# Splitting one output store into 112 + 4 + 4 + 4 + 4 rows in a linear-attention kernel on one core

## The chip, the core and the metric

The kernel runs on one core of a Trainium2 chip. Five engines work side by side: PE (TensorE, matrix multiplies; PEld is its weight load), DVE (VectorE), ACT (ScalarE), POOL (GpSimd) and SP (SyncE). SP, ACT and POOL also issue DMA transfers, and all transfers of the core run on the same 16 DMA engines. The metric is the time of one execution on the device, in microseconds (us).

## The reference

For 8 x 12 = 96 heads of 512 positions and 64 features, all float32, it computes linear attention with a ReLU feature map:

```python
Q_feat = np.maximum(0, Q)
K_feat = np.maximum(0, K)
KV = np.einsum('bhkd,bhkv->bhdv', K_feat, V)
K_sum = np.sum(K_feat, axis=2)
numerator = np.einsum('bhqd,bhdv->bhqv', Q_feat, KV)
denominator = np.einsum('bhqd,bhd->bhq', Q_feat, K_sum)
return (numerator / (denominator[:, :, :, None] + 1e-10)).astype(np.float32)
```

Q, K and V are 12.58 MB each, 37.75 MB read in all, and the output is 12.58 MB.

## The kernel before

**Tiling.** Heads are taken eight at a time: an "octet", and there are NO = 12 of them, numbered by `o`. A quantity of one octet is 1 MB in float32. K and V of an octet come as two groups of four heads, each a tile of 128 partitions x 16 rows x 64 features; Q of an octet is one tile of 128 partitions x 32 rows x 64. The output tile `o_sb` of an octet is 128 partitions x 32 rows x 64 in float32, so one partition ("row" of the transfer) holds 2048 numbers, 8 KB, which are contiguous in DRAM.

**Loads.** K and V of octet 0 are loaded as float32, by SP (`k_first`) and ACT (`v_first`), into two buffers of the pool of output tiles. All other loads are issued by POOL in the order Q0, K1, V1, Q1, K2, V2, Q2 ... and turn float32 into bf16 on the way (lines 94 and 106). They have their own buffers, and each POOL load waits until an earlier one has landed, so that some eight are under way at a time.

**Compute.** Per group DVE makes the ReLU of K (`kf`, line 138) and copies of V (`vo`, lines 140, 147; ACT does some, line 145). PE multiplies them into `ps_kv` (line 152), ACT moves the result to `kvd` (line 162). Q is transposed on PE (line 173), ACT applies the ReLU (line 181). PE makes the denominators (line 212) and the transposed numerators (line 203), ACT copies these (line 205), PE transposes them back (line 230), and DVE multiplies by the reciprocals and writes `o_sb` (line 236). `backs(o)` is that last part for octet `o`, and it ends in `store(o, o_sb)`.

**Stores.** All stores are issued by SP (line 249, and line 247 for the last octet, whose store is cut in two halves along the free axis). SP works its instructions off in order. With `DELAY = 6`, store `o` of the first six octets also waits for the landing of K load `o + 6` (line 251): it is kept back so that the loads come first. The pool `outp` has DELAY + 2 = 8 buffers, so the tile of octet 8 takes the buffer of octet 0 (two of the eight were used first by `k_first` and `v_first`), and its writer has to see that octet 0's store has landed. The order of all instructions is the order in which the program text issues them (`manual_schedule`); a framework adds the semaphores.

Of the kernel before, what the change touches and what calls it, by code (L numbers as in the profile page):

```python
# [10 lines left out]
def kernel(  # L11
# [7 lines left out]
    nc = tc.nc  # L19
    B, H, S, D = Q.shape  # L20
    assert D == 64
    P = 128
# [9 lines left out]
    NO = NG // 2  # L32
    assert NO * 8 == NH and R == 16 and RQ == 32
    DELAY = 6
# [54 lines left out]
    k_load = {}  # L89
    after_load = mybir.DependencyInfo(mybir.DependencyClass.Sync, mybir.DependencyReason.DATA)  # L90
# [151 lines left out]
    def store(o, o_sb):  # L242
        Ov = Or[o].rearrange("p (r d) -> p r d", d=D)
        if o == NO - 1:
            for j in range(2):
                rs = slice(RQ // 2 * j, RQ // 2 * (j + 1))
                nc.sync.dma_start(out=Ov[:, rs], in_=o_sb[:, rs])
            return
        st = nc.sync.dma_start(out=Ov, in_=o_sb)
        if o + DELAY < NO:  # L250
            tc.add_manual_dep(st.ins, k_load[o + DELAY].ins.name, after_load, reason="store after load")

    def out_tile():
        return outp.tile([P, RQ, D], fp32, name="o_sb", tag="o_sb")
# [19 lines left out]
    def backs(o):  # L274
        o_sb = out_tile()
        for j in range(2):
            norm(o, j, back(o, j), o_sb)
        store(o, o_sb)
# [26 lines left out]
    o = NO - 2  # L305
# [10 lines left out]
    o_sb = out_tile()  # L316
# [4 lines left out]
    for i in range(2):  # L321
        relu_q(o + 1, i, transp(o + 1, i), nc.vector if i == 1 else None)
    norm(o, 1, ps, o_sb)
    store(o, o_sb)
    idle(5, o + 1)
    out_t(o + 1, (0,))
# [32 lines left out]
```

## Time and profile before

| What | Value |
|---|---|
| Median of 3 runs | 127.03 us (126.72 to 127.13) |
| The profiled execution | 127.0 us, of which the span of the instructions is 125.2 |
| Busy: PE, PEld, DVE, ACT, POOL | 85.0, 76.9, 81.0, 79.0, 23.7 us |
| DMA | 10139 packets, 32.66 MB on the core's side |
| Queue q0 (POOL's loads) | 74.1% of 16 engines' span |
| Queue q1 (SP: first K load and all stores) | 27.1% |
| Queue q8 (instruction fetches) | 8 packets |
| One 1024 KB store, issue to landing | 8.9 us in the median |

The page divides the span into 40 slices; a digit is the busy share in tenths. "DMA" is the mean share over the 16 DMA engines. [...] A DMA transfer raises a semaphore 16 times, once for each DMA engine, and "landed" means that all 16 have come.

### The profile page before, as it was taken

The page shows a single profiled execution, that of the slowest core. Times are in us where ns is not written, and L with a number is a line of the kernel's source. Part 1 is how long each engine was busy: PE and PEld are TensorE (multiplying, and loading weights), DVE is VectorE, ACT ScalarE, POOL GpSimd, SP SyncE. Part 2 cuts the span into 40 slices and gives each one's busy share as a digit, 9 for nine tenths or more (in the row PEclk, how much of TensorE's full clock was granted, in tenths as well). Part 3 has the DMA queues.
Part 4 walks back from the last instruction along what each step waited for, and adds up shares of the span by engine and source line. Part 5 has one row for each costly group of instructions (what it writes and reads, how often), then busy time and mean ns, then how long its engine had stood idle before and what let it go on. Part 6 is the DMA issues. An engine that isn't in the chain of part 4 may idle for free.

```text
span 125.2 us, 2614 instructions
## 1 busy us (share of the span) xinstructions
PE 85.0 (68%) x1067; PEld 76.9 (61%) x1067; DVE 81.0 (65%) x176; ACT 79.0 (63%) x114; POOL 23.7 (19%) x40
## 2 busy tenths in 40 slices
PE   0000547898989979898966985955997597797600
PEld 0000547796878879787855983943975595775500
DVE  2006963679889797979859349449549409978610
ACT  0003737999899898989877576845499095547000
POOL 6922124221242213322121130210000000000000
PEclk9999999999999999999999599996899869999996
DMA  3999999999999999999999999999999999999991
GB/s 92 365 306 229 215 209 211 213 211 217 207 217 208 211 213 211 214 273 311 214 247 341 210 222 342 234 217 325 258 215 305 279 215 307 425 419 419 432 403 73
DMA packets 10139, 32.66 MB, mean 261 GB/s; under 512 B 784, under 2 KB 784, under 8 KB 8720
## 3 DMA queue, kind: packets, MB, share of 16 engines
q0 software_dynamic: 7712, 17.83, 74.1%
q1 hardware_dynamic: 2144, 13.63, 27.1%
q10 hardware_dynamic: 272, 1.05, 2.2%
q8 instruction: 8, 0.13, 0.4%
q14 instruction: 3, 0.02, 0.0%
HBM read 37.75 MB, written 12.58 MB: 402 GB/s over the span
## 4 chain that ended last, share of the span: by engine, by line
DVE 37%; DMA 28%; PE 19%; ACT 7%; issue 3%; DVEq 1%; ACTq 0%
DMA v_sb<-in_V_dram 20%; DVE o_sb L236 15%; PE ps_kv L152 10%; DMA k_first<-in_K_dram 7%; DVE kf L138 7%; PE ps_bk L230 7%; DVE vo L140 4%; ACT kvd L162 3%; DVE vo L147 3%; DVE den L220 2%; PE ps_qt L173 2%; DVE rec L224 2%; DVE own L215 2%; ACT qt L181 2%; ACT vo L145 1%
## 5 line engine op out<-in xcount | busy, mean ns | idle before, releaser
L152 PE MATMUL ps_kv<-vo,kf 128*128 128x132 bf16 x384 | 30.2, 240 | 19.9 <-ACT vo L145 13.8
L152 PEld LDWEIGHTS <-kf 128*128 128x128 bf16 x384 | 27.4, 107 | 21.6 <-DVE vo L140 12.9
L236 DVE TENSOR_TENSOR o_sb<-ps_bk,rec 128x1024 f32<-128x1024 f32 x24 | 28.3, 1219 | 13.6 <-PE ps_bk L230 13.6
L162 ACT CAST kvd<-ps_kv 64x260 bf16<-64x260 f32 (+1 forms) x54 | 18.6, 345 | 16.6 <-PE ps_kv L152 13.9
L205 ACT COPY ot_sb<-ps_ot 128x1024 f32<-128x1024 f32 x24 | 24.1, 1013 | 6.8 <-PE ps_ot L203 5.9
L230 PE MATMUL ps_bk<-ident,ot_sb 128*128 128x128 f32 x192 | 23.4, 276 | 0.4 <-ACT ot_sb L205 0.4
L181 ACT ACTIVATE qt<-ps_qt 128x1024 bf16<-128x1024 bf16 x23 | 22.4, 1028 | 0.2
L230 PEld LDWEIGHTS ps_bk<-ident,ot_sb 128*128 128x128 f32 x192 | 21.2, 143 | 0.7 <-ACT ot_sb L205 0.7
L203 PE MATMUL ps_ot<-qt,kvd 128*128 128x256 bf16 x96 | 14.9, 283 | 9.9 <-DVE o_sb L236 9.0
L138 DVE TENSOR_SCALAR kf<-k_sb,mask 128x1024 bf16<-128x1024 bf16 x44 | 18.4, 459 | 4.5 <-DMA k_sb<-in_K_dram 4.5
L203 PEld LDWEIGHTS <-kvd 128*128 128x128 bf16 x96 | 9.2, 100 | 13.2 <-issue 11.0
L173 PE MATMUL ps_qt<-ident,q_sb 128*128 128x128 bf16 x192 | 14.7, 237 | 0.7 <-DMA q_sb<-in_Q_dram 0.7
L173 PEld LDWEIGHTS <-q_sb 128*128 128x128 bf16 x192 | 13.3, 108 | 1.4 <-DMA q_sb<-in_Q_dram 1.3
L140 DVE TENSOR_SCALAR vo<-v_sb,mask 128x1024 bf16<-128x1024 bf16 x22 | 11.0, 501 | 4.7 <-DMA v_sb<-in_V_dram 4.7
L145 ACT ACTIVATE vo<-v_sb,mask 128x1024 bf16<-128x1024 bf16 x10 | 11.5, 1154 | 2.0 <-DMA v_sb<-in_V_dram 1.8
L94 POOL DMA_DIRECT2D v_sb<-in_V_dram x11 | 8.2, 750 | 22.2 <-DMA q_sb<-in_Q_dram 9.4
L106 POOL DMA_DIRECT2D q_sb<-in_Q_dram x12 | 7.1, 588 | 20.9 <-DMA k_sb<-in_K_dram 15.3
L94 POOL DMA_DIRECT2D k_sb<-in_K_dram x11 | 7.9, 717 | 15.4 <-DMA v_sb<-in_V_dram 9.8
L212 PEld LDWEIGHTS <-qt 128*128 128x128 bf16 x192 | 6.8, 96 | 3.6 <-ACT qt L181 2.5
L212 PE MATMUL ps_den<-kvd,qt 128*128 128x16 bf16 x192 | 7.3, 180 | 1.9 <-ACT qt L181 1.7
L145 ACT ACT_TABLE_LOAD x1 | 1.3, 1283 | 11.3 <-DMA v_first<-in_V_dram 11.3
L138 DVE TENSOR_SCALAR kf<-k_first,mask 128x1024 bf16<-128x1024 f32 x4 | 2.8, 750 | 7.7 <-DMA k_first<-in_K_dram 7.7
(24 smaller groups left out, 31.8 us busy)
## 6 DMA issues: line engine op xcount, KB each, us to landing
out_dram<-o_sb SPq DMA_DIRECT2D x11, 1024.0 KB, 8.9
q_sb<-in_Q_dram POOLq DMA_DIRECT2D x12, 512.0 KB, 20.7
k_sb<-in_K_dram POOLq DMA_DIRECT2D x11, 512.0 KB, 21.8
v_sb<-in_V_dram POOLq DMA_DIRECT2D x11, 512.0 KB, 20.5
k_first<-in_K_dram SPq DMA_DIRECT2D x1, 1024.0 KB, 9.3
v_first<-in_V_dram ACTq DMA_DIRECT2D x1, 1024.0 KB, 10.5
out_dram<-o_sb SPq DMA_DIRECT2D x2, 512.0 KB, 4.5
```

The lines of the kernel that those rows point to most:

```text
L94: ld = eng.dma_start(out=t.rearrange("p g r d -> p g (r d)"), in_=X[2 * o:2 * o + 2].rearrange("g p f -> p g f"))
L138: nc.vector.tensor_scalar(kf[g][:, :, s, :], k_sb[g], scalar1=0.0, scalar2=mask[:, 0, s:s + 1], op0=Alu.max, op1=Alu.mult)
L140: nc.vector.tensor_scalar(vo[g % NB][:, :, 0, 2:D + 2], v_sb[g], scalar1=mask[:, 1, 0:1], scalar2=None, op0=Alu.mult)
L152: nc.tensor.matmul(ps_kv[:, g % 2, 0:2 * (D + 2)].rearrange("p (t d) -> p t d", t=2), kf[g][:, r, :, :].rearrange("p s d -> p (s d)"), vo[ ...
L162: copy(kvd[o % NK][64 * c:64 * c + 64, 4 * gs.start + s:4 * gs.stop:2, c * D1:c * D1 + D1].rearrange("p (g t) d -> p g t d", t=2), ps_kv[6 ...
L173: nc.tensor.transpose(ps[:, u, :], q_sb[o][:, i * (U // 2) + u, :], ident)
L181: nc.scalar.activation(to, ps, Act.Relu)
L203: nc.tensor.matmul(ps[:, i], kvd[o % NK][:, h, 1:2 * D + 1], q[:, :, h, :], start=True, stop=True, skip_group_check=True)
L205: nc.scalar.copy(ot[o][:, :, 4 * j:4 * j + 4], ps.rearrange("p h u c -> p u h c"))
L212: nc.tensor.matmul(ps[:, u], qt_sb[o % NZ][:, u, :], kvd[o % NK][:, :, 0:2 * D1:2 * D1 - 1], start=True, stop=True, skip_group_check=True)
L230: nc.tensor.transpose(ps[:, 2 * v:2 * v + 2].rearrange("p c d -> p (c d)"), ot[o][:, 8 * j + v].rearrange("p h c -> p (h c)"), ident32)
L236: nc.vector.tensor_tensor(o_sb[:, rs], ps, rec[o][:, rs].unsqueeze(2).to_broadcast([P, 16, D]), op=Alu.mult)
```

## The change

The store of octet 0 is issued as five transfers, along the partitions: rows 0 to 111, 112 to 115, 116 to 119, 120 to 123 and 124 to 127. All five carry the same wait for K load 6. The other stores are as before. A transfer's rows are divided among DMA engines: 128 rows are 8 for each of the 16, 112 rows are 7 for each of the 16, and 4 rows are 1 for each of 4 engines. By the change's description these four are engines 0 to 3, which then carry 11 rows of octet 0's store while the others carry 7. Bytes and results are the same.

```diff
@@ store()
                 rs = slice(RQ // 2 * j, RQ // 2 * (j + 1))
                 nc.sync.dma_start(out=Ov[:, rs], in_=o_sb[:, rs])
             return
-        st = nc.sync.dma_start(out=Ov, in_=o_sb)
-        if o + DELAY < NO:
-            tc.add_manual_dep(st.ins, k_load[o + DELAY].ins.name, after_load, reason="store after load")
+        cuts = [0, 112, 116, 120, 124, P] if o == 0 else [0, P]
+        for lo, hi in zip(cuts, cuts[1:]):
+            st = nc.sync.dma_start(out=Ov[lo:hi], in_=o_sb[lo:hi])
+            if o + DELAY < NO:
+                tc.add_manual_dep(st.ins, k_load[o + DELAY].ins.name, after_load, reason="store after load")
```

## The prediction

> **What bounds the kernel now.** First the page: its slices, DMA queues and chain.
>
> ```profile
> span 125.2 us, 2614 instructions
> ...
> DMA  3999999999999999999999999999999999999991
> GB/s 92 365 306 229 215 209 211 213 211 217 207 217 208 211 213 211 214 273 311 214 247 341 210 222 342 234 217 325 258 215 305 279 215 307 425 419 419 432 403 73
> ...
> q0 software_dynamic: 7712, 17.83, 74.1%
> q1 hardware_dynamic: 2144, 13.63, 27.1%
> q10 hardware_dynamic: 272, 1.05, 2.2%
> q8 instruction: 8, 0.13, 0.4%
> ```
>
> The 16 DMA engines are full from the second slice to the last but one. PE, DVE and ACT are at 63 to 68% of the span. The chain of work names DVE, DMA and PE in turn, but it ends on the last compute instruction, and the stores land after that. So I cut the end into windows:
>
> ```profile
> core 0: us, PE busy (x) PEld busy (x) DVE busy (x) ACT busy (x) POOL busy (x), PEclk, DMA share, GB/s
> ...
> 104.00:122.00 18.00, 11.13 (x140) 9.51 (x136) 12.80 (x23) 6.66 (x11) 0.00 (x0) 1.00 1.01 408
> 122.00:123.00 1.00, 0.00 (x0) 0.00 (x0) 0.00 (x0) 0.00 (x0) 0.00 (x0) 1.00 0.55 221
> 123.00:124.00 1.00, 0.00 (x0) 0.00 (x0) 0.00 (x0) 0.00 (x0) 0.00 (x0) 0.50 0.07 29
> ```
>
> From 104 to 122 us there are only stores, back to back; then the engines stop one after another. In the trace's DMA records a transfer's landing is 16 increments, one per engine: those of the last store come at 122.14, 122.20, 122.21 and 122.27 us, and so on to 123.89. The slowest DMA engine sets the end, and the first four finish 1.6 to 1.75 us before it.
>
> The records also show where that spread is from. The landing increments of a load at 25.98 us spread over 0.7 us. Then the q8 row's eight instruction fetches follow, 16 KB each, one packet of 879 to 974 ns on one engine (starts 26.95, 36.74, 47.78, 57.91, 70.58, 83.24, 98.31, 111.56). After each, one more engine lands about 0.9 to 1.1 us late and stays so: one at 29.29, two at 39.2, three at 51.66, some eight at the end.
>
> Now the store that changes, in SP's waits and then its timeline:
>
> ```profile
> SPq L249 <- DMA k_sb<-in_K_dram: 98.5, 6, 50.5
> ```
>
> ```profile
> 51.74 0.35 SPq L249 DMA_DIRECT2D out_dram<-o_sb  x1
> 61.67 0.33 SPq L249 DMA_DIRECT2D out_dram<-o_sb  x1
> ```
>
> Store 0 leaves at 51.74, as soon as K load 6 has landed (51.66), store 1 at 61.67. By the records, store 0's rows start at 55.16, 8 KB per packet, 8 per engine, alternating with load packets (309 to 322 ns a row, 154 a load packet), and it lands at 60.68.
>
> **The change part by part.** *Issues.* One DMA instruction becomes five. SP takes four more at 0.33 to 0.35 us, so 1.4 us: the fifth leaves near 53.2, before the first row moves (55.16) and 8.4 us before store 1 is due. Cost nothing; the cover is SP's wait for K load 7. POOL's queue is not touched. *Waits.* All five wait for the same K load, so the last four find it done: an event wait of 17 ns each. *Semaphores.* Landings rotate over eight in the records. Four more transfers shift the rotation, and the tightest reuse becomes the last store's (at 119.4), which needs the semaphore of store 4, landed at 100.64. Nothing waits. *Buffer.* Octet 8's multiply on DVE (92.39) reuses octet 0's tile and must see five landings, not one; they are there by about 63. At 21 ns an event wait that is 0.08 us of DVE, covered by the DMA backlog.
>
> *Rows.* This is the whole price. An engine that serves rows one after another needs 0.306 us for each (8 rows of a 1 MB store, 2.45 us between landings in the tail). Twelve engines get 7 rows for 8: -0.31 us. Engines 0 to 3 get 11: +0.92 us, if the four rows of a piece move at the speed of other rows. Four more completion packets at 22 ns add 0.09 us to each.
>
> *Do they?* Every store of before is one transfer of 128 rows, and there a row takes 309 to 322 ns. In a piece four engines at once read four neighbouring partitions, a form that the trace does not show. Lower end: fully parallel, four pieces take 4 x 0.309 = 1.24 us per engine. Upper end: neighbouring rows are served one after another, so that each piece takes 4 x 0.309 = 1.24 us and four take 4.94. The engines' extra is then between +0.92 and +4.63 us. A stretched packet does hold its engine: after the fetch at 57.91 a store row took 755 ns and the next load packet began only at its end. A reason for a gain below 0.92 I see none. I take about +2.3: four engines that collide on the first piece leave it at different times, and are then partly on different pieces, which are different partitions. It lies nearer the parallel end, where the rows I have are.
>
> [...]
>
> [...]
>
> *Sum.* Last landing of before: 123.89 in a span of 125.2, in an execution of 127.0; the median of the three runs shown is 127.03, so the sum is carried over as it is. Engines 4 to 15: 123.89 - 0.31 = 123.58. Engines 0 to 3, if they are early ones: 122.2 to 122.5 + 2.3 = 124.5 to 124.8, say 124.7. The later sets the end: +0.8 us, **127.8 us**. What is late next: the loads that land between 60 and 104 us come up to 1.4 us later, because engines 0 to 3 are now the last; compute (DVE's waits on loads of 1.6 to 2.1 us) moves with them, but it has no say in the end: the last multiply ends at 118.2 while rows are queued until 121.
>
> **The rivals.** *A. Parallel and well aimed.* Rows of a piece cost 0.31 each and all four engines are among the early ones: 122.2 to 122.6 + 1.0 = 123.2 to 123.6, the others 123.58. End -0.3: **126.7 us** (own range 126.5 to 126.9). It decides wherever engines 0 to 3 have over 1.3 us in hand and a piece takes under about 0.4 us. For it: four engines do end 1.6 us early, and 3 rows for 4 engines is just that size. Against it: it needs both conditions.
>
> *B. Parallel but badly aimed.* One of engines 0 to 3 is one of the eight late ones, which land the last store between 123.05 and 123.89. Then 123.1 to 123.9 + 0.95: **127.2 to 128.0 us**, say 127.6. The records carry no engine number. I followed each engine's packets end to start back to the first transfer, whose 16 first packets start 14 ns apart, and took that order for the numbers. Of the first four, one leads to an engine that later had a fetch (83.24 or 111.56). Through the stalls of the first microseconds that is half a coin toss.
>
> *C. Full collision.* Serial pieces: engines 0 to 3 +4.6, end 122.2 + 4.6 = 126.8, +2.9: **130 us**. Also what comes out if a piece goes to one engine, always the same. The spread-out arrival speaks against the whole of it.
>
> *D. It does not do what it says:* the rows are spread over other engines, or a third thing sets the end; 127.0, within 0.2.
>
> **How the numbers follow.** Partial collision (the forecast) 0.43, at 127.4 to 128.8; A 0.20; B 0.22; C 0.04; D 0.11. A change of 0.3% (0.38 us) is about what a measurement of this kernel can tell from none. Faster by more: 0.08 of A, whose -0.3 is at the edge, 0.04 of D: 0.12. Within: 0.12 of A, 0.05 of D, 0.05 of B, 0.04 of the forecast: 0.26. Slower: the rest, 0.62. The range leaves out C, half of A's faster half and the upper end of the forecast's: 126.6 to 129.1; the forecast's own is 127.4 to 128.8.
>
> **What would show it.** The issue list should have x10 of 1024 KB, one of 896 and four of 32. If a piece uses four engines, q1 has 2160 packets (112 + 16 completions + 4 x 8 for 128 + 16); 2208 if each uses sixteen. Collision: some 8 KB packets of q1 between 56 and 62 us that take 0.6 to 1.2 us. A well-aimed rebalance: the last store's landings within less than 1.2 us instead of 1.75. The prediction is wrong if the pieces' rows take 0.31 us, and the sign then hangs on whether engines 0 to 3 had fetches; the windows after 122 us show it as a steeper or a longer tail.

## The result, and the profile after

The changed kernel takes 127.70 us in the median of 4 runs (127.61 to 127.92), against 127.00 us for the kernel before (126.72 to 127.13, 4 runs). The ratio is 1.0061, 95% interval 1.0040 to 1.0082: slower by 0.6%, or 0.7 us. The profiled execution took 127.71 us, with a span of 125.9 us (before: 127.0 and 125.2).

The page of the changed kernel, the lines that answer to those shown of before, with two lines of its list of DMA issues (count, KB of one, median us from issue to landing):

```profile
span 125.9 us, 2620 instructions
...
DMA  3999999999999999999999999999999999999990
...
q0 software_dynamic: 7712, 17.83, 73.6%
q1 hardware_dynamic: 2160, 13.63, 26.8%
q10 hardware_dynamic: 272, 1.05, 2.2%
q8 instruction: 8, 0.13, 0.4%
q14 instruction: 3, 0.02, 0.0%
...
out_dram<-o_sb SPq DMA_DIRECT2D x2, 512.0 KB, 6.6
out_dram<-o_sb SPq DMA_DIRECT2D x1, 896.0 KB, 7.6
```

q1 has 2160 packets for 2144: each small transfer adds four completion packets, so each goes to four DMA engines. In the records a small transfer raises its semaphore not 16 times but five: once between 52.59 and 53.66 us, before any row of the store moves (55.13), and four times as its rows land (59.37 to 59.48 for the first, 61.25 to 61.41 for the last). The engines are full for as long as before. What is new lies behind the last full slice. The end of the changed kernel in windows of half a microsecond (the last two columns are the DMA share and GB/s):

```profile
122.00:122.50 0.50, 0.00 (x0) 0.00 (x0) 0.00 (x0) 0.00 (x0) 0.00 (x0) 0.50 0.78 320
122.50:123.00 0.50, 0.00 (x0) 0.00 (x0) 0.00 (x0) 0.00 (x0) 0.00 (x0) 0.50 0.45 180
123.00:123.50 0.50, 0.00 (x0) 0.00 (x0) 0.00 (x0) 0.00 (x0) 0.00 (x0) 0.50 0.12 49
123.50:124.00 0.50, 0.00 (x0) 0.00 (x0) 0.00 (x0) 0.00 (x0) 0.00 (x0) 0.50 0.04 16
```

The same two last windows of the kernel before:

```profile
123.00:123.50 0.50, 0.00 (x0) 0.00 (x0) 0.00 (x0) 0.00 (x0) 0.00 (x0) 0.51 0.14 57
123.50:124.00 0.50, 0.00 (x0) 0.00 (x0) 0.00 (x0) 0.00 (x0) 0.00 (x0) 0.50 0.00 0
```

After 123.5 us before moves nothing more. After the change something still moves at 16 GB/s and 4% of 16 engines: that is one engine, alone. In the records the last store's 16 landing increments read 122.01, 122.12, 122.44 and so on up to 123.56 and 123.57, and then one by itself at **124.35**. The other fifteen end 0.32 us before the last increment of before (123.89). So the change did most of what it says, and one of the four loaded engines spoils it.

That is +0.46 us (124.35 - 123.89), and the loss is 0.71. The rest comes after the last landing. SP ends the program by waiting for the stores' semaphores. Its waits from 118 us on, before and then after (us in total, times, longest):

```profile
SPq L354 <- DMA out_dram<-o_sb: 3.8, 3, 1.4
```

```profile
SPq L356 <- DMA out_dram<-o_sb: 6.1, 3, 3.7
```

The records give these waits an order: semaphores 108, 109, 113, 114, 115, 116, 117, 118, whatever landed last, about 0.06 us apart even where a wait finds its store done. In before the last store raises semaphore 117; SP passes it at 123.91, has one more to look at, and ends (its drain) at 124.03, 0.14 us after the landing. Four more transfers turn the rotation of eight on, and the last store raises 113. SP passes that at 124.36, must still go through 114 to 118, one by one, at 124.43, .48, .55, .61 and .67, and drains at 124.73, 0.38 us after the landing. That is +0.25 us, and 0.46 + 0.25 = 0.71.

### The profile page after: what moved, and what is told of

The parts are those of the page before. It is cut to its first block, busy times and chain, and to the rows that moved or that the text cites. A ratio compares the mean times of both kernels' runs of the same rounds, so it can differ in the third digit from the quotient of the medians.

```text
span 125.9 us, 2620 instructions
## 1 busy us (share of the span) xinstructions
PE 83.8 (67%) x1067; PEld 75.9 (60%) x1067; DVE 80.9 (64%) x176; ACT 79.1 (63%) x114; POOL 23.4 (19%) x40
## 3 DMA queue, kind: packets, MB, share of 16 engines
q1 hardware_dynamic: 2160, 13.63, 26.8%
q10 hardware_dynamic: 272, 1.05, 2.2%
## 4 chain that ended last, share of the span: by engine, by line
DVE 35%; DMA 28%; PE 22%; ACT 5%; issue 2%; DVEq 1%; ACTq 0%
DMA v_sb<-in_V_dram 21%; DVE o_sb L236 15%; PE ps_kv L152 10%; DMA k_first<-in_K_dram 7%; PE ps_bk L230 7%; DVE kf L138 6%; DVE vo L140 4%; ACT kvd L162 3%; PE ps_qt L173 3%; DVE vo L147 2%; DVE den L220 2%; PE ps_ot L203 2%; DVE rec L224 2%; DVE own L215 2%; ACT qt L181 2%
## 5 line engine op out<-in xcount | busy, mean ns | idle before, releaser
L152 PE MATMUL ps_kv<-vo,kf 128*128 128x132 bf16 x384 | 28.9, 235 | 20.5 <-ACT vo L145 13.8
L152 PEld LDWEIGHTS <-kf 128*128 128x128 bf16 x384 | 26.3, 104 | 22.0 <-DVE vo L140 12.9
L173 PE MATMUL ps_qt<-ident,q_sb 128*128 128x128 bf16 x192 | 15.2, 242 | 0.5 <-DMA q_sb<-in_Q_dram 0.5
L173 PEld LDWEIGHTS <-q_sb 128*128 128x128 bf16 x192 | 13.8, 111 | 1.3 <-DMA q_sb<-in_Q_dram 1.1
```

Source lines behind the costliest of these rows:

```text
L152: nc.tensor.matmul(ps_kv[:, g % 2, 0:2 * (D + 2)].rearrange("p (t d) -> p t d", t=2), kf[g][:, r, :, :].rearrange("p s d -> p (s d)"), vo[ ...
L173: nc.tensor.transpose(ps[:, u, :], q_sb[o][:, i * (U // 2) + u, :], ident)
```

## The experiments

All kernels are the changed one with other cuts, except one that is the kernel before. "Before" is timed beside them: 126.93 us (126.71 to 127.17, 31 runs) for the first four, 127.07 (126.66 to 127.64, 30 runs) for the next four, 127.03 (126.68 to 127.35, 24 runs) for the last three.

The theories that the expectations name: *one late engine* (or *late engine*): the rows cost 0.31 us each, and one of the loaded engines has lost its margin to a fetch. *Check order*: the extra waits of SP behind the last landing. *Collision*: engines that read neighbouring partitions slow each other, as the prediction had it. *Price per transfer*: each further transfer costs something by itself. *Uneven start*, in the last group only: the engines are already apart before any store is issued.

One table holds the readings. The first column of times is the mean landing increment of the load that lands at about 21 us, long before a store is issued; then that of the last store; then by how much the slowest engine is behind that mean; then the time from the last landing to the end of the execution. Start + 102.46 + lag + tail is the time of each profiled execution: between the start and the end the mean engine needs 102.45 to 102.48 us in all of these kernels, so work per core is the same, and only its division, the start and the tail differ.

| Kernel (cuts of octet 0) | start | mean end | lag | tail | profiled | median | ratio, 95% |
|---|---|---|---|---|---|---|---|
| before | 20.55 | 123.03 | 0.86 | 3.11 | 127.00 | 127.0 | 1 |
| before, second profile | 20.75 | 123.20 | 0.71 | 3.09 | 127.00 | 127.06 | 1.0000 (0.9989 to 1.0011) |
| changed (112, 4, 4, 4, 4) | 20.61 | 123.06 | 1.29 | 3.36 | 127.71 | 127.70 | 1.0061 (1.0040 to 1.0082) |
| e1 (112, 16) | 20.63 | 123.08 | 0.77 | 3.03 | 126.88 | 126.98 | 1.0002 (0.9993 to 1.0012) |
| e2 (112, 3, 3, 3, 7) | 20.43 | 122.89 | 0.46 | 3.38 | 126.73 | 126.95 | 1.0004 (0.9994 to 1.0014) |
| e3 (112, 2, 2, 2, 10) | 20.72 | 123.19 | 0.59 | 3.33 | 127.11 | 127.09 | 1.0011 (1.0001 to 1.0020) |
| e4 (112, 1, 1, 1, 13) | 20.73 | 123.18 | 0.64 | 3.35 | 127.17 | 127.09 | 1.0013 (1.0004 to 1.0023) |
| e5 (64, 16, 16, 16, 16) | 20.48 | 122.95 | 0.59 | 3.37 | 126.92 | 126.89 | 0.9984 (0.9973 to 0.9995) |
| e6 (e2, octet 1 in five) | 20.44 | 122.92 | 0.63 | 3.11 | 126.66 | 126.67 | 0.9966 (0.9953 to 0.9980) |
| e7 (changed, octet 1 in five) | 20.51 | 122.97 | 1.25 | 3.11 | 127.32 | 127.45 | 1.0027 (1.0016 to 1.0038) |
| e8 (64, 32, 32) | 20.53 | 123.00 | 0.72 | 3.47 | 127.19 | 127.01 | 0.9994 (0.9982 to 1.0006) |
| e10 (e5, octet 1 likewise) | 20.52 | 122.98 | 0.72 | 3.11 | 126.81 | 126.76 | 0.9971 (0.9960 to 0.9983) |
| e11 (112, 4, 4, 8) | 20.42 | 122.87 | 1.21 | 3.43 | 127.51 | 127.40 | 1.0025 (1.0016 to 1.0034) |

### Which rows cost: one, two or three engines loaded, or none

e1: one extra transfer, every engine keeps its eight rows.

```diff
-        cuts = [0, 112, 116, 120, 124, P] if o == 0 else [0, P]
+        cuts = [0, 112, P] if o == 0 else [0, P]
```

> Octet 0's store as two transfers of 112 and 16 rows, so that every DMA engine has 8 rows as before. One-late-engine theory (only the number of rows per engine counts, and one of engines 0 to 3 has no time in hand): 127.0 us, within 0.2 of before; rows of the second transfer take 0.31 to 0.32 us. Collision theory (engines that read neighbouring rows at once slow each other): the 16-row transfer has four engines on each four neighbours, so rows of 0.4 to 1.2 us and 127.3 to 128. A price per transfer would show as up to a quarter of the change's +0.7, so 127.2.

Measured: 126.98 us, ratio 1.0002; last landing 123.85, as in before. A first piece of 112 rows and one more transfer cost nothing that can be measured.

e2: pieces of three rows and a last one of seven. Engines 0 to 2 carry 11 rows, 3 to 6 eight, the others seven.

```diff
-        cuts = [0, 112, 116, 120, 124, P] if o == 0 else [0, P]
+        cuts = [0, 112, 115, 118, 121, P] if o == 0 else [0, P]
```

> Five transfers of 112, 3, 3, 3 and 7 rows: engines 0 to 2 have 11 rows, 3 to 6 have 8, 7 to 15 have 7. One-late-engine theory: if the late engine is 0, 1 or 2, its last landing stays at 124.3 us and the time at 127.7; if it is engine 3, its 3 rows less are 0.92 us, the end goes to the others, at 123.6 to 123.9, and the time to 126.7 to 127.1. Collision theory: three engines collide in place of four, 127.4 to 127.7.

Measured: 126.95 us, ratio 1.0004. The windows of its end:

```profile
122.50:123.00 0.50, 0.00 (x0) 0.00 (x0) 0.00 (x0) 0.00 (x0) 0.00 (x0) 0.50 0.31 123
123.00:123.50 0.50, 0.00 (x0) 0.00 (x0) 0.00 (x0) 0.00 (x0) 0.00 (x0) 0.50 0.00 0
```

The last landing is at 123.35, one whole microsecond before that of the changed kernel, with the same number of transfers and three of the same four engines loaded in the same way. So neither the transfers nor 11 rows on engines 0 to 2 make the late landing: it is the fourth engine, number 3. (That a piece of n rows goes to engines 0 to n-1 is how the change is described. The 16 further packets of the changed kernel show four engines for a piece of four; which engines they are was not shown, since the records carry no engine number.) The time is no better than before, although the landing is 0.54 us earlier in the profiled execution: 0.27 of this is lost in the tail, 3.38 for 3.11, and the median of ten runs shows nothing of the rest.

e3 and e4: two engines, and one engine, with 11 rows.

```diff
-        cuts = [0, 112, 116, 120, 124, P] if o == 0 else [0, P]
+        cuts = [0, 112, 114, 116, 118, P] if o == 0 else [0, P]
```

> Five transfers of 112, 2, 2, 2 and 10 rows: engines 0 and 1 have 11 rows, 2 to 9 have 8, 10 to 15 have 7. One-late-engine theory: 127.7 if the late engine is 0 or 1, otherwise 126.9 to 127.1 (late engines among 2 to 9 keep their 8 rows, so the end can hardly fall below that of before). Collision theory: two engines collide, 127.2 to 127.5.

```diff
-        cuts = [0, 112, 116, 120, 124, P] if o == 0 else [0, P]
+        cuts = [0, 112, 113, 114, 115, P] if o == 0 else [0, P]
```

> Five transfers of 112, 1, 1, 1 and 13 rows: engine 0 has 11 rows, 1 to 12 have 8, 13 to 15 have 7. One-late-engine theory: 127.7 if the late engine is engine 0, otherwise 127.0. Collision theory: nothing collides in the one-row transfers, 127.0 in any case; slower only by what the 13-row transfer costs, up to 127.3.

Measured: 127.09 us both, ratios 1.0011 and 1.0013. The last landings are 123.78 and 123.82, and no engine is alone at the end (lag 0.59 and 0.64). Five transfers together with their longer tail (3.33 and 3.35) therefore cost some 0.15 us here, 0.3 at most by the intervals, and the loss does not grow step by step with the engines loaded: it is there with four and not with three.

### What makes engine 3 late

The lone landing can be followed back from store to store. In the changed kernel the last increment of octet 8's store is at 116.23 and that of octet 9's at 119.47: 3.24 us apart, where 2.45 is the usual distance. From there on one engine is alone. In between lies one fetch. The DMA view of the changed kernel from 117 to 118.5 us (packets, MB, share of 16 engines):

```profile
q1 hardware_dynamic: 90, 0.63, 101.2%
q14 instruction: 1, 0.01, 1.3%
```

(Packet times over 16 engines' span pass 100% elsewhere too: q0 alone has 109.2% from 30 to 36 us in the kernel before.) The q14 packet starts at 117.41, has 8 KB and takes 309 ns, and the store row right after it takes 659 ns where its neighbours take 309. Together that is 0.31 + 0.35 = 0.66 us of the at least 0.79 (3.24 - 2.45) that this engine falls back; what the other 0.13 are was not found. The records name no engine, but packets can be followed from the end of one to the start of the next, with eight rows to a store: from the row behind the fetch the path with the evenest gaps leads to the last packet of all, here and in e11 and e7 (below). In e2, where the fetch comes at 117.27, it leads to an engine that ends before the last. e11 has the same thing at another time, and takes one of the four rows away from engine 3.

```diff
-        cuts = [0, 112, 116, 120, 124, P] if o == 0 else [0, P]
+        cuts = [0, 112, 116, 120, P] if o == 0 else [0, P]
```

> Octet 0 as 112, 4, 4 and 8 rows: engines 0 to 3 carry ten rows of it, 4 to 7 eight, 8 to 15 seven, and the last transfer's semaphore is 109, with six checks behind it. Theory late engine plus check order: engine 3 has one row of 0.31 us less than in the changed kernel, its landing at 124.35 - 0.31 = 124.04 us if its two 8 KB fetches come as before, and DRAIN 0.43 us behind it, so 124.04 + 3.42 = 127.45 us. Late engine alone: 127.4 as well, but with the tail of before, 127.15. Collision: 127.5, two thirds of the changed kernel's loss being gone with two of its three long runs of four rows left.

Measured: 127.40 us, ratio 1.0025; last landing 124.08 (expected 124.04), tail 3.43 (expected 3.42). The end in windows, and SP's waits from 118 us on:

```profile
123.00:123.50 0.50, 0.00 (x0) 0.00 (x0) 0.00 (x0) 0.00 (x0) 0.00 (x0) 0.50 0.06 25
123.50:124.00 0.50, 0.00 (x0) 0.00 (x0) 0.00 (x0) 0.00 (x0) 0.00 (x0) 0.50 0.02 8
```

```profile
SPq L356 <- DMA out_dram<-o_sb: 4.5, 2, 3.4
```

One engine is alone again, with 8 GB/s in the last window instead of 16. Its late 8 KB fetch starts at 118.68 (309 ns, the store row behind it 659 ns). The store that landed just before that fetch, at 118.40, has a slowest engine only 0.52 us behind the mean; the next, at 121.64, again 3.24 us later, 1.26 us. So up to the fetch none of the loaded engines was late: the extra rows had fitted into their margin, and the fetch took it away. e7, below, shows it a third time, with the fetch at 110.58: last landings 108.78 and 112.03, 3.25 us apart. (There a 16 KB fetch, at 109.90, lies in the same stretch; in the other two kernels none does.)

In the kernel before, the same fetch comes at 122.05 us (121.96 in its second profile), within the last store. Its DMA view from 117 to 125 us has it:

```profile
q14 instruction: 1, 0.01, 0.2%
```

The engine that carries it is late there without being the last. Of the 16 increments of the last transfer but one, seven come early (to 121.43, the next at 121.76); of the last transfer only six do (to 122.67, the next at 123.05). By this the fetch meets an early engine in before too, but one that has not given its margin to extra rows.

### The tail

e5: five transfers, but each engine keeps its eight rows. The last store raises semaphore 113, as in the changed kernel.

```diff
-        cuts = [0, 112, 116, 120, 124, P] if o == 0 else [0, P]
+        cuts = [0, 64, 80, 96, 112, P] if o == 0 else [0, P]
```

> Octet 0 as 64, 16, 16, 16 and 16 rows: five transfers as in the changed kernel, but every DMA engine carries the same eight rows as before. Theory check order (the semaphore of the last transfer is 113 in place of 117, and SP checks five more semaphores behind it instead of one, 0.06 us each): the last landing stays near 123.9 us, DRAIN comes 0.37 us after it instead of 0.12 to 0.14, and the time is 127.0 + 0.25 = 127.2 us. Theory late engine alone (only rows per engine and fetches count): 127.0. Theory price per transfer: 127.7, as the changed kernel.

Measured: 126.89 us, ratio 0.9984. The tail is what was expected, 3.37 us, with the drain 0.38 us after the landing. The time is not: 0.3 us lower than expected. In the profiled execution the last landing is at 123.55, 0.34 before that of before. Of this, 0.08 is there before any store is issued (mean end 122.95 for 123.03, as the start), and 0.27 is a smaller lag. No theory on record expected that.

e8: three transfers, eight rows on each engine, the last store on semaphore 108, the first in SP's order.

```diff
-        cuts = [0, 112, 116, 120, 124, P] if o == 0 else [0, P]
+        cuts = [0, 64, 96, P] if o == 0 else [0, P]
```

> Octet 0 as 64, 32 and 32 rows: every engine keeps its eight rows, and the last transfer's semaphore is 108, the first in SP's order, with seven checks behind it. Theory check order: DRAIN 0.13 + 6 x 0.06 = 0.5 us after the last landing, 127.0 + 0.37 = 127.35 us, more than with five transfers although there are fewer. Late engine alone: 127.0. Price per transfer: half of the price of the five, so less than with five.

Measured: 127.01 us, ratio 0.9994. SP's waits from 118 us on:

```profile
SPq L356 <- DMA out_dram<-o_sb: 5.6, 1, 5.6
```

One wait where before has three: SP stands at the first semaphore of its order until everything has landed, and then goes through the other seven. Drain 0.51 us after the landing, tail 3.47, as expected. The median, again, is 0.34 under the expectation.

e10: e5 with octet 1 cut in the same way, so that the last store is back on 117.

```diff
-        cuts = [0, 112, 116, 120, 124, P] if o == 0 else [0, P]
+        cuts = [0, 64, 80, 96, 112, P] if o < 2 else [0, P]
```

> Octets 0 and 1 both as 64, 16, 16, 16 and 16 rows: eight rows of each octet on every engine, and the last transfer's semaphore is 117 with one check behind it. Theory check order: as the kernel with five even transfers (126.89 us) less 0.25 us, 126.65, with 3.1 us from the last landing to the end of the execution. If the five even transfers were faster than their expectation for another reason that goes with the number of transfers, it is not 0.25 us away from them: 126.9 or above.

Measured: 126.76 us, ratio 0.9971, tail 3.11. Four transfers more than e5, and the tail is 0.26 us shorter, not longer; the landing was 0.15 later in the profiled execution. In the medians the step is 0.13 us, less than the 0.25 expected.

The drain follows the last landing by 0.08 us with no semaphore behind the last one (118: e1), 0.14 with one (117: before, e10), 0.38 with five (113: changed, e5), 0.45 with six (109: e11) and 0.51 with seven (108: e8). That is 0.08 + 0.06 each, in kernels with 13 to 21 stores, so it goes by the place in the order and not by the number of transfers.

### Both terms taken apart, and a faster kernel

e7: the change itself, with octet 1 in five even pieces, which brings the last store back to 117 and leaves the rows of octet 0 alone.

```diff
-        cuts = [0, 112, 116, 120, 124, P] if o == 0 else [0, P]
+        cuts = {0: [0, 112, 116, 120, 124, P], 1: [0, 64, 80, 96, 112, P]}.get(o, [0, P])
```

> The change itself, and octet 1 as 64, 16, 16, 16 and 16 rows: the last transfer's semaphore is 117 again, rows per engine are those of the changed kernel. Theory check order plus late engine: engine 3 still lands alone near 124.35 us, the check behind it is short, 127.7 - 0.25 = 127.45 us. Late engine alone: 127.7. Check order alone: 127.0.

Measured: 127.45 us, ratio 1.0027, last landing 124.21, tail 3.11. The end in windows:

```profile
123.00:123.50 0.50, 0.00 (x0) 0.00 (x0) 0.00 (x0) 0.00 (x0) 0.00 (x0) 0.50 0.06 25
123.50:124.00 0.50, 0.00 (x0) 0.00 (x0) 0.00 (x0) 0.00 (x0) 0.00 (x0) 0.50 0.04 16
```

The lone engine is there, and the tail of before is back: 3.11 us for 3.36 in the changed kernel. The median is 0.25 us below that of the changed kernel.

e6: the same filling, with the three-row pieces of e2.

```diff
-        cuts = [0, 112, 116, 120, 124, P] if o == 0 else [0, P]
+        cuts = {0: [0, 112, 115, 118, 121, P], 1: [0, 64, 80, 96, 112, P]}.get(o, [0, P])
```

> Octet 0 as 112, 3, 3, 3 and 7 rows (as the three-row kernel, 126.95 us with its last landing at 123.35) and octet 1 as 64, 16, 16, 16 and 16, which gives every engine its eight rows of octet 1 and brings the last transfer's semaphore round to 117, with one check behind it. Theory check order: the landing stays near 123.4 us and DRAIN comes 0.12 to 0.14 us after it, so 126.95 - 0.25 = 126.7 us, faster than the kernel before. Late engine alone: 126.95, no change. Price per transfer: slower than 127.0 by what eight further transfers cost.

Measured: 126.67 us, ratio 0.9966 (0.9953 to 0.9980). This is faster than both kernels. How much of it the aimed rows are worth is not shown: e10, with even rows and the same tail, is at 0.9971, well inside the interval.

### How much the start moves

e9: the kernel before, with no edit.

> The kernel before, unchanged, profiled a second time. Theory uneven start (one engine is already 0.45 us behind the mean at the load that lands at 21 us in the first profile of before, 0.18 us in the kernel with five even transfers, and keeps that to the end): if the lag belongs to the kernel, it is again 0.4 to 0.5 us at 21 us, the last landing near 123.9 us and the late 8 KB instruction fetch again near 122 us; if it belongs to the execution, it differs, and the last landing with it. Time 127.0 either way, no difference.

Measured: 127.06 us, ratio 1.0000. The last landing is at 123.91 and the late 8 KB fetch at 121.96, so both came again in a second execution. The start does not stay: 20.75 us instead of 20.55, with the slowest engine 0.37 us behind the mean instead of 0.45. Over all profiles the start lies between 20.42 and 20.75. All of that is over 30 us before the first store is issued, so no cut of a store causes it directly.

**What stays open.** e5, e8 and e10 have even rows, and their medians are 0.44, 0.42 and 0.27 us below that of before plus the change of their tails. Their profiles show a start that is 0.02 to 0.27 us earlier and a lag 0.27 smaller to 0.01 larger than in the two profiles of before, not one clear place. Whether it is the arrangement of the program, the place of the fetches or the shorter transfers of octet 0 was not found. Nor does a run show why the late 8 KB fetch meets engine 3, or change the engine that it meets: that the fetch takes the margin rests on its time, which moved from 117.41 to 118.68 and 110.58 while the lone landing moved with it.

## Why the prediction was right, and where it was not

The number was right: 127.8 forecast, 127.70 measured, slower as said. Its reason was not, and that they meet is luck. The sum was 0.8 us, all of it a later last landing (124.7) through colliding rows; measured are 0.46 for the landing (124.35), by rows at their plain price and a fetch, and 0.25 behind it, which the sum had at nothing. By the prediction's own sign, "wrong if the pieces' rows take 0.31 us", its mechanism has failed: they took 0.32. What it said would then decide, "whether engines 0 to 3 had fetches", did decide.

**Rows and collision: the step that failed.** "I take about +2.3: four engines that collide on the first piece" is wrong; the changed kernel shows no collision, and the right value was the lower end, +0.92 and 0.09 for completions. The DMA view from 55 to 62 us, before and then after:

```profile
q1 hardware_dynamic: 144, 1.05, 37.5%
```

```profile
q1 hardware_dynamic: 160, 1.05, 37.3%
```

The same 1.05 MB, 16 completion packets more, and no more engine time: sixteen rows of 1.2 us in place of 0.31 would have raised the share by 14 of 112 engine-microseconds, some 13 points. In the records the rows of the four pieces start at 58.58 to 58.69, 59.21 to 59.31, 59.84 to 59.94 and 60.47 to 60.57, and the longest of the 8 KB store packets between 56 and 62 us takes 322 ns. So here four engines read four neighbouring partitions at once without slowing each other. The four pieces are 4 x 0.32 = 1.29 us on each engine, side by side, where the upper end of the prediction had 4.94.

**Rival B had the form, with another culprit.** "Parallel but badly aimed", 127.2 to 128.0, is what happened: the rows cost their parallel price and one of the four engines is late. It is late from an 8 KB q14 fetch and the row it stretches (0.66 us), not from one of the eight 16 KB fetches that B spoke of. The prediction counted those eight and never looked at q14, whose three packets stand on the page of before as well. An early engine, 122.2 to 122.6, plus 1.0 for rows and 0.66 for the fetch and its row is 123.9 to 124.3, or 124.0 to 124.4 with the 0.79 by which that engine fell back; 124.35 was measured. (The late engines were also miscounted: ten of the 16 increments of before, not eight, lie between 123.05 and 123.89.)

**Rival A fits engines 0 to 2.** In the changed kernel they land no later than 123.57, and A said 123.2 to 123.6; which landings are theirs the records do not tell. With three-row pieces all engines are in by 123.35. With aimed rows A's time of 126.7 was reached only when the tail was that of before, in e6.

**Twelve engines with seven rows.** "-0.31 us" gave 123.58; the fifteen engines that are not late end at 123.57.

**Semaphores: the step that was missed.** "Four more transfers shift the rotation ... Nothing waits" is true of reuse and wrong as a price. The shift decides how many waits are left behind the last store, and that is +0.25 us, shown by e7 against the changed kernel and by the tails of e1, e5, e8 and e11.

**Issues and waits.** The five issues of the changed kernel, by line (ns min/median/max, first and last start in us):

```profile
L251 SPq DMA_DIRECT2D out_dram<-o_sb x5: 260/326/358, 51.7 to 53.2; - x5
L251 SPq EVENT_SEMAPHORE  x1: 17/17/17, 51.6 to 51.6; - x1
```

They leave by 53.2 us, as worked out, and cost nothing; there is one event wait, not five.

**What is late next.** Loads and compute were to move up to 1.4 us later. They did not, since nothing collided: stores 1 to 5, which wait for K loads 7 to 11, leave at 61.67, 71.61, 81.56, 91.50 and 101.45 us, against 61.67, 71.62, 81.57, 91.52 and 101.75 before. The start of the last two issues, before and then after:

```profile
118.23 1.46 SPq L247 DMA_DIRECT2D out_dram<-o_sb  x2
```

```profile
116.63 1.46 SPq L247 DMA_DIRECT2D out_dram<-o_sb  x2
```

The last store is issued 1.6 us earlier than before (0.8 us earlier than in the second profile of before, so half of this differs from execution to execution), and it makes no difference: rows are queued until 121 us anyway, as the prediction said of the end.

**Two small readings.** A load packet beside store 0's rows takes 172 to 173 ns in the records, not 154; no term of the sum uses it. And the range 126.6 to 129.1 holds the whole of the forecast's own, 127.4 to 128.8, though it is said to leave out its upper end.

## What to carry to other kernels

Where the DMA engines set the end, split the time into start, mean engine, slowest engine and tail; here the cuts of a store worked on the last two, and the mean engine stayed within 0.03 us. Before loading "early" engines, list every fetch on every queue, the short ones too: the margin that was read at the end of the kernel before already had the eight 16 KB fetches in it, and one 8 KB fetch that came late in the changed kernel took 0.66 us of it, with the row behind it. When the number of transfers changes, look at which semaphore the last one raises and how many waits stand behind it: four transfers more, elsewhere, gave 0.25 us back here (127.70 to 127.45 us, e7).

## What the runs showed of the hardware

- Four DMA engines that read 8 KB rows of four neighbouring partitions took 322 ns each in the changed kernel, like the other 8 KB rows between 55 and 62 us of its trace (309 to 322).
- The late 8 KB instruction fetch took 309 ns, and the 8 KB store row behind it 649 to 662 ns instead of 309 in the changed kernel (659) and in all ten of its variants. In the kernel before, where the fetch fell among the 4 KB rows of the last store, the row behind it took 367 ns (372 in the second profile) instead of 159.
- The time of that fetch went with the number of SP's stores: 122.0 us with 13, 119.2 with 14, 117.3 to 118.7 with 15 to 17, and 110.6 to 112.2 with 21. What it fetched was not shown.
- At the end of the program SP went through the semaphores of the stores in the same order in these kernels, at 0.06 us each, and its drain came 0.08 us (e1) to 0.51 us (e8) behind the last landing.
